# The last token group's output and query products on whole float32 operands instead of rounded high and low halves

## The chip, the cores and the metric

The kernel runs on one core of one Trainium2 chip. The metric is the device time of one execution in microseconds (us); less is better. A core has a matrix engine (TensorE, in the profile PE; its weight loads are PEld), a vector engine (VectorE, DVE), an activation engine (ScalarE, ACT), GpSimd (POOL) and SyncE (SP), which issues most transfers. Each engine takes its instructions in the order in which they stand in its queue.

## The reference, cut to what matters

One decoder layer over 1024 tokens of width 1024: a layer norm, a mixer of eight attention heads and four recurrent heads, an output projection, a layer norm, and PEER retrieval over 16384 experts, of which each token uses 128.

```python
mixed = jnp.concatenate([fox_o, h_o], axis=-1)
mix = mixed @ w_out                                  # output product, 1024 x 1024
x = _layer_norm(DEEPNORM_ALPHA * x + mix, ...)
q = (xt @ w_q).reshape(T, PEER_HEADS, 2, PEER_HALF)  # query product, 1024 x 2048
s = jnp.einsum('thpd,hpnd->thpn', q, sub_keys)
s_top, i_top = lax.top_k(s, PEER_TOPK)               # 16 of 128, per head and half
```

All of it is float32.

## The kernel before

The tokens go through the mixer in three groups (`GROUPS`): tokens 0 to 255, 256 to 767 and 768 to 1023. For each group the kernel runs the attention (`fox`) and the recurrence (`hgrn`), then the output product and the layer norm (`mix_out`), then the query product, the scores and their top 16 (`select`). This text is about the last group, 256 tokens.

A product of two float32 matrices is made of three matrix products in the format float32r, which keeps fewer bits (`mm3`). A weight tile of 128x1024 comes from memory (`wraw`); ScalarE rounds it (`whi`), and another engine forms the rest (`wlo`) by a subtraction. For the last group `WDIV` gives 1 for both products, which sends every such subtraction to GpSimd:

```python
nc.scalar.activation(hi, raw, AF.Copy)
self.nw += 1
eng = nc.vector if not WDIV[k] or self.nw % WDIV[k] else nc.gpsimd
eng.tensor_tensor(lo, raw, hi.bitcast(F32), op=ALU.subtract)
```

The other operand is held in `mh` and `ml`, the same two halves of the mixer's output and later of its layer norm; `ml` is formed by VectorE wherever `mh` is written. `mm3` adds high by high, high by low and low by high. The last group's output product takes 8 weight tiles, 64 products of 128x128 by 128x256 counted without their halves; its query product takes 16 tiles and 128 products. The raw tiles have 3 buffers, the halves 3 each (`WRAW`, `weight`). Products that are not split, such as the attention's logits (line 667), its sums over values (line 704) and the scores (line 822), are fed with whole float32 operands already.

While the last group is in its mixer, output product and selection, another job runs between its steps: `gbuild` writes the gates of four token blocks (`DENSE`) as a dense matrix `d_g`. It has 64 steps of eight tokens. In a step VectorE makes 16-bit one-hot tiles of 128x1024 (line 947: `ohi`, `ohj`, `ah`, `al`; every other step ScalarE makes `ah`), TensorE multiplies them (lines 972 and 974), and ScalarE copies the result to `slab`. Four steps fill a slab of 2 MB, of which there is one buffer; it must be written out before the next is begun. `tick` decides how many of these steps are put between two steps of the main work, by the constants `RATE`, in the program's text, not at run time. What is left of them when the selection is issued is drained after it.

After that the dense stage begins (`dense`): all 16384 experts for the four dense blocks as matrix products, and beside it the rest of the gather of expert rows for the other blocks. It is not touched. The order of instructions on each engine is fixed when the program is built; tiles are given places in the on-chip memory as pools open and close on its left and right side, and a load into a place waits for the last use of what was there.

Of the kernel before, what the change touches and what calls it, by code (L numbers as in the profile page):

```python
# [8 lines left out]
F32 = mybir.dt.float32  # L9
F32R = mybir.dt.float32r  # L10
# [5 lines left out]
ALU = mybir.AluOpType  # L16
# [4 lines left out]
P = 128  # L21
DC = D // P
# [30 lines left out]
FPOST = {256: 2, 512: 2}  # L53
WRAW = {"p0": 3, "m0": 3, "s0": 3, "p1": 3, "m1": 3, "s1": 3, "m2": 3, "s2": 3}
EARLY = 0
LNB = {256: 0, 512: 2}
HKD, HXK, HSB = 1, (), ()
PLAG = 1
# [13 lines left out]
class Layer:  # L72
# [130 lines left out]

    def weight(self, wp, src, k):
        nc = self.nc
        raw = wp.tile([P, 1024], F32, name="wraw", tag="wraw", bufs=WRAW[k])
        hi = wp.tile([P, 1024], F32R, name="whi", tag="whi", bufs=3)
        lo = wp.tile([P, 1024], F32R, name="wlo", tag="wlo", bufs=3)
        self.q("w").dma_start(raw, src)
# [4 lines that stand above are left out]
        return hi, lo  # L214
# [49 lines left out]
    def transpose_split(self, st, src, hi, lo, t, pool=None):  # L264
        nc = self.nc
        sl = slice(t * P, (t + 1) * P)
        for c0 in range(0, DC, 4):
            pt = self.bank(st)
            for c in range(4):
                nc.tensor.transpose(pt[:, c * P : (c + 1) * P], src[:, (c0 + c) * P : (c0 + c + 1) * P], self.ident)  # L270
            v = pt.rearrange("p (c t) -> p c t", c=4)
            h = hi[:, c0 : c0 + 4, sl]
            nc.scalar.activation(h, v, AF.Copy)
            if pool:
                x = pool.tile([P, 4, P], F32, name="tsx", tag="tsx", bufs=2)
                nc.scalar.activation(x, v, AF.Copy)
                nc.gpsimd.tensor_tensor(lo[:, c0 : c0 + 4, sl], x, h.bitcast(F32), op=ALU.subtract)
            else:
                nc.vector.tensor_tensor(lo[:, c0 : c0 + 4, sl], v, h.bitcast(F32), op=ALU.subtract)

    def mm3(self, out, lh, ll, rh, rl, start, stop, **kw):
        mm = self.nc.tensor.matmul
        mm(out, lh, rh, start=start, stop=False, **kw)  # L283
        mm(out, lh, rl, start=False, stop=False, **kw)  # L284
        mm(out, ll, rh, start=False, stop=stop, **kw)  # L285

    def projT(self, w, xh, xl, T):
        wh, wl = (t.rearrange("p (c m) -> p c m", c=DC) for t in w)
        out = []
        for c0 in range(0, T, 512):  # L290
            c = min(T - c0, 512)
            po = self.bank("h" if c0 else "f")[:, :c]
            for dc in range(DC):
                self.mm3(po, wh[:, dc], wl[:, dc], xh[:, dc, c0 : c0 + c], xl[:, dc, c0 : c0 + c], dc == 0, dc == DC - 1)
            out.append((slice(c0, c0 + c), po))
        return out

    def projN(self, wp, name, g, xh, xl, nq, k):
        po = [self.bank("h" if n == 2 else "f").rearrange("p (b n) -> p b n", b=2) for n in range(nq // 2)]
        for half in range(2):  # L300
            w = self.weight(wp, self.a[name][g, half], k)
            wh, wl = (t.rearrange("p (c n) -> p c n", c=4) for t in w)
            for tb in range(nq):
                for c in range(4):
                    dc = half * 4 + c
                    ts = slice(tb * P, (tb + 1) * P)
                    self.mm3(po[tb // 2][:, tb % 2], xh[:, dc, ts], xl[:, dc, ts], wh[:, c], wl[:, c],
                             dc == 0 and tb % 2 == 0, dc == DC - 1, skip_group_check=True)
        return po

    def mixers(self, groups, es):
        st, gb, tl = ExitStack(), ExitStack(), ExitStack()
        self.lx = ExitStack()
        init = self.setup()
        next(init)
        x1 = self.project(*groups[0], st)
        next(init)
        for n, (t0, T) in enumerate(groups):
            nq = T // P
            late = n + 1 == len(groups)  # L320
            if n < 2:
                self.project_cols(t0, T if n == 0 else S - t0, *x1)
            st.close()
            if n < 2:
                tl.close()
            po = st.enter_context(self.pool("po", 1, "left"))
            mh = po.tile([P, DC, T], F32R, name="mh", tag="mh")
            ml = po.tile([P, DC, T], F32R, name="ml", tag="ml")
            with self.pool("pf", 1, "left") as pf, self.pool("pk", 2, "left") as pk, \
                    self.pool("pg", 2, "left") as pg:  # L330
                fx = self.fox(t0, T, mh, ml, pf, pk)
                hg = self.hgrn(t0, T, mh, ml, pg)
                for _ in range(nq):
                    next(hg)
                    for i in range(8 // nq):
                        if i == HPOST[T]:
                            next(hg)
                        next(fx)
                    if HPOST[T] >= 8 // nq:
                        next(hg)  # L340
                    self.tick("hgrn", T)
            self.mix_out(t0, T, mh, ml)
            while late and not self.tailed:
                next(self.bjobs[0])
            pz = self.pz if late else tl.enter_context(self.pool("pz", 1, "right"))
            sv = pz.tile([P, nq, 16, 16], F32, name="sv", tag="sv")
            si = pz.tile([P, nq, 16, 16], U32, name="si", tag="si")
            best = pz.tile([P, nq, 8, 16], F32, name="best", tag="best")
            pos = pz.tile([P, nq, 8, 16], U32, name="pos", tag="pos")
            if n == 0:  # L350
                x1 = self.preload(T, S - T)
            self.select(t0, T, mh, ml, sv, si, best, pos, T == 256 or EARLY)
            if late:
                self.drain(self.bjobs)
                gb.close()
                st.close()
                while self.nv < sum(b not in VDVE for b in GATHER):
                    self.tick("dense")
                self.hx.close()
                dense = self.dense_prep(es)  # L360
            pw = tl.enter_context(self.pool("pw", 1, "right"))
            if n == 0:
                x1 = self.project(T, S - T, st, x1)
                self.lx.close()
            tail = self.select_tail(t0, T, sv, si, best, pos, T == 256 or EARLY, pw)
            if T == 256:
                tail = self.tail_gather(t0, T, tail)
                if late:
                    return dense, tail, tl
                self.drain([tail])  # L370
                self.hold = HOLD
            else:
                self.tailed = False
                self.bjobs.append(self.tail_gbuild(tail, tl, gb))
# [114 lines left out]
    def hgrn(self, t0, T, mh, ml, pg):  # L489
        nc = self.nc  # L490
# [7 lines left out]
        for ck in range(T // P):  # L498
            r0 = t0 + ck * P
            rs = slice(r0, r0 + P)  # L500
            q, f, v, k, lf = t4("q", QB[T]), t4("f", QB[T]), t4("v", QB[T]), t4("k", 2), t4("lf")
# [40 lines left out]
            for li, c in ((-2, 64), (-1, 32), (0, 16), (1, 8), (2, 4), (3, 2)):  # L542
# [12 lines left out]
                                        op=ALU.mult)  # L555
# [15 lines left out]
                else:  # L571
# [4 lines left out]
                                    op=ALU.mult)  # L576
# [9 lines left out]
            pt = b4()  # L586
# [12 lines left out]
            for h in range(4):  # L599
                nc.vector.scalar_tensor_tensor(self.state[:, h], self.state[:, h], eb[:, h : h + 1], pst[:, h],  # L600
                                               op0=ALU.mult, op1=ALU.add)
# [16 lines left out]
            pt = b4()  # L618
            for h in range(4):
                nc.tensor.transpose(pt[:, h], ov[:, h], self.ident)  # L620
            sl = slice(ck * P, (ck + 1) * P)
            nc.scalar.activation(mh[:, 4:8, sl], pt, AF.Copy)
            nc.vector.tensor_tensor(ml[:, 4:8, sl], pt, mh[:, 4:8, sl].bitcast(F32), op=ALU.subtract)
            yield

    def fox(self, t0, T, mh, ml, pf, pk):
        nc = self.nc
# [58 lines left out]
        def mixv(h, prs):  # L686
            p, e = divmod(h, 2)
# [27 lines left out]
            if e == 1:  # L715
# [8 lines left out]
                def post():  # L724
                    po = self.bank("f")[:, :T]
                    for qb in range(nq):
                        nc.tensor.transpose(po[:, qb * P : (qb + 1) * P], o[:, qb], self.ident)
                    g = self.foxg[:, p : p + 1]
                    nc.scalar.activation(mh[:, p], po, AF.Copy, scale=g)
                    nc.vector.scalar_tensor_tensor(ml[:, p], po, g, mh[:, p].bitcast(F32), op0=ALU.mult, op1=ALU.subtract)  # L730
                    self.dump("mh", mh[:, p].bitcast(F32), lambda d: d[p * P : (p + 1) * P, t0 : t0 + T])

                if FPOST[T] and h < 7:
# [568 lines left out]
```

## Time and profile before

| | |
|---|---|
| median of 3 runs | 3122.69 us (3122.61 to 3125.11) |
| the profiled execution, its time | 3098.22 us |
| its span | 3096.5 us |
| busy PE / PEld / DVE / ACT / POOL | 2614.4 / 2150.2 / 2707.3 / 1097.2 / 1678.8 us |
| mean granted clock of TensorE | 0.918 of full speed |

The profiled execution was 24.5 us faster than the median of the timed runs; all rows below come from it. Times in rows are us from the start of the span, unless marked ns. A row of a timeline with a count of x5 stands for five instructions in a row; an instruction's duration reaches into that of the next where the engine overlaps them, so a pace is read from start to start.

### The profile page before, as it was taken

The numbers are of one execution on the slowest core, as the hardware profiler recorded it, in microseconds if no ns is written. First come the engines' busy times: TensorE is split into PE (matmuls) and PEld (weight loads), VectorE is DVE, ScalarE is ACT, GpSimd is POOL, SyncE is SP. The second block draws the span as 40 slices with busy tenths as digits, with TensorE's granted clock in tenths as the row PEclk, the third lists the DMA queues.
The fourth block names the chain that finished last, engine by engine and source line by source line (L and its number), as shares of the span: only waits on it lengthen the run. The fifth ranks groups of instructions, "written<-read, shape, count | busy, mean of one in ns | idle before, by whom it ended". The sixth has DMA issues, their size and how long they took to land.

```text
span 3096.5 us, 45624 instructions
## 1 busy us (share of the span) xinstructions
PE 2614.4 (84%) x16057; PEld 2150.2 (69%) x16057; DVE 2707.3 (87%) x5573; ACT 1097.2 (35%) x2028; POOL 1678.8 (54%) x1240
## 2 busy tenths in 40 slices
PE   6778799777779768777569999899989999999995
PEld 6768589755566545666457778687768877877874
DVE  8658766588769998989798999899999999999998
ACT  4733222365222433766322223232323322222331
POOL 2344377655656644433046666565567665656652
PEclk9878899898889889879689999999999999999997
DMA  7632599754978858763489999999999999999994
GB/s 269 198 137 89 184 336 330 241 162 151 350 253 290 290 164 298 256 249 144 186 280 342 346 377 360 340 366 361 350 344 367 381 379 357 357 370 342 370 336 159
DMA packets 338662, 887.13 MB, mean 286 GB/s; under 512 B 29912, under 2 KB 124136, under 8 KB 336000
## 3 DMA queue, kind: packets, MB, share of 16 engines
q0 software_dynamic: 147456, 536.94, 47.5%
q1 hardware_dynamic: 185200, 338.38, 31.3%
q10 hardware_dynamic: 5776, 8.90, 0.8%
q8 instruction: 126, 2.06, 0.3%
q14 instruction: 104, 0.85, 0.1%
HBM read 821.67 MB, written 62.42 MB: 286 GB/s over the span
## 4 chain that ended last, share of the span: by engine, by line
DVE 40%; PE 36%; issue 11%; DMA 6%; ACT 4%; POOL 3%; SPq 0%; DVEq 0%; POOLq 0%; ACTq 0%
DVE ys L1134 8%; DVE rows L1109 6%; PE psf L284 6%; PE psf L285 5%; PE psf L283 5%; PE psh L285 4%; PE psh L283 4%; PE psh L284 4%; DMA rows<-in_v,gsel 2%; POOL rows L1090 2%; DVE dy L1049 2%; DVE vl L1017 1%; DVE ohj L947 1%; DVE tw L793 1%; DVE al L947 1%
## 5 line engine op out<-in xcount | busy, mean ns | idle before, releaser
L1090 POOL DMA_INDIRECT rows<-in_u,gsel x512 | 689.7, 1347 | 481.8 <-DVE rows L1109 302.5
L1090 POOL DMA_INDIRECT rows<-in_v,gsel x512 | 637.9, 1246 | 433.3 <-DVE ys L1134 264.5
L1109 DVE SCALAR_TENSOR_TENSOR rows<-rows,gx 128x1024 f32<-128x1024 f32 x512 | 629.8, 1278 | 38.6 <-DMA rows<-in_u,gsel 25.3
L1134 DVE SCALAR_TENSOR_TENSOR ys<-rows,sd,ys 128x1024 f32<-128x1024 f32 x381 | 491.2, 1289 | 0.6
L283 PE MATMUL psh<-dxh,uh 128*128 128x512 f32 x1024 | 402.8, 393 | 28.9 <-ACT uh L1016 16.1
L285 PE MATMUL psh<-dxh,ul 128*128 128x512 f32 x1024 | 400.8, 391 | 9.5 <-DVE ul L1017 9.4
L284 PE MATMUL psh<-dxl,uh 128*128 128x512 f32 x1024 | 400.3, 391 | 0.0
L284 PE MATMUL psf<-vl,hh 128*128 128x512 f32 x768 | 312.3, 407 | 42.9 <-DVE vl L1017 42.1
L1016 ACT ACTIVATE vh<-vr 128x512 fp32r<-128x512 f32 x256 | 161.8, 632 | 435.8 <-PE psv L285 408.7
L285 PE MATMUL psf<-vh,hl 128*128 128x512 f32 x768 | 307.7, 401 | 0.0
L283 PE MATMUL psf<-vh,hh 128*128 128x512 f32 x768 | 279.1, 395 | 11.9 <-DVE dy L1049 9.7
L1016 ACT ACTIVATE uh<-ur 128x1024 fp32r<-128x1024 f32 x128 | 136.0, 1062 | 410.6 <-PE psh L284 408.9
L213 POOL TENSOR_TENSOR wlo<-wraw,whi 128x1024 fp32r<-128x1024 f32 x70 | 181.8, 2603 | 154.1 <-ACT whi L210 145.7
L283 PEld LDWEIGHTS psh<-dxh,uh 128*128 128x128 f32 x1024 | 193.5, 189 | 76.8 <-ACT hs L1030 20.3
L285 PEld LDWEIGHTS psh<-dxh,ul 128*128 128x128 f32 x1024 | 193.4, 189 | 50.6 <-DVE ul L1017 10.5
L210 ACT ACTIVATE whi<-wraw 128x1024 fp32r<-128x1024 f32 x130 | 136.9, 1056 | 250.8 <-PE psf L284 64.1
L284 PEld LDWEIGHTS psh<-dxl,uh 128*128 128x128 f32 x1024 | 193.6, 189 | 39.7
L284 PEld LDWEIGHTS psf<-vl,hh 128*128 128x128 f32 x768 | 148.7, 194 | 90.2 <-DVE vl L1017 59.4
L1017 DVE TENSOR_TENSOR vl<-vr,vh 128x512 fp32r<-128x512 f32 x256 | 170.6, 688 | 14.0 <-ACT vh L1016 13.9
L283 PEld LDWEIGHTS psf<-vh,hh 128*128 128x128 f32 x768 | 145.5, 190 | 50.1 <-DVE dy L1049 10.0
L213 DVE TENSOR_TENSOR wlo<-wraw,whi 128x1024 fp32r<-128x1024 f32 x60 | 81.8, 1365 | 111.0 <-ACT whi L210 111.0
L285 PEld LDWEIGHTS psf<-vh,hl 128*128 128x128 f32 x768 | 149.1, 194 | 30.2
(337 smaller groups left out, 6354.4 us busy)
## 6 DMA issues: line engine op xcount, KB each, us to landing
ur<-in_ut SPq DMA_DIRECT2D x128, 512.0 KB
vr<-in_v SPq DMA_DIRECT2D x256, 256.0 KB
d_g<-slab SPq DMA_DIRECT2D x16, 2048.0 KB
gt<-d_g SPq DMA_DIRECT2D x32, 1024.0 KB
wraw<-in_wq SPq DMA_DIRECT2D x48, 512.0 KB
wraw<-in_wt SPq DMA_DIRECT2D x34, 512.0 KB
wraw<-in_wn SPq DMA_DIRECT2D x24, 512.0 KB
wraw<-in_wo SPq DMA_DIRECT2D x24, 512.0 KB
```

The source lines that it names most:

```text
L210: nc.scalar.activation(hi, raw, AF.Copy)
L213: eng.tensor_tensor(lo, raw, hi.bitcast(F32), op=ALU.subtract)
L283: mm(out, lh, rh, start=start, stop=False, **kw)
L284: mm(out, lh, rl, start=False, stop=False, **kw)
L285: mm(out, ll, rh, start=False, stop=stop, **kw)
L947: eng.tensor_tensor(t.rearrange("p t (m c) -> p t m c", c=2), x, y, op=op)
L1016: nc.scalar.activation(hi, raw, AF.Copy)
L1017: nc.vector.tensor_tensor(lo, raw, hi.bitcast(F32), op=ALU.subtract)
L1049: nc.vector.tensor_tensor(y[:, tb, ns], y[:, tb, ns], acc[tb], op=ALU.add)
L1090: self.nc.gpsimd.indirect_dma_start(out=t, out_offset=None, in_=tab, in_offset=bass.IndirectOffsetOnAxis(ap=idx, axis=0))
L1109: self.pin(nc.vector.scalar_tensor_tensor(u, u, 1.0, x2, op0=ALU.mult, op1=ALU.mult, accum_out=sd[:, n : n + 1]), "u")
L1134: self.pin(nc.vector.scalar_tensor_tensor(ys, v, h, ys, op0=ALU.mult, op1=ALU.add), "w")
```

## The change

The last group's two products, `m2` and `s2`, are named in a table `WHOLE` with the number of buffers of their raw tiles, 5 and 6. For them `weight` issues the load alone; `mm3` issues one matrix product on the raw tile and on an `mh` of type float32; `ml` isn't allotted, and the four places that form it are skipped. The other two groups are as before.

```diff
+WHOLE = {"m2": 5, "s2": 6}
...
     def weight(self, wp, src, k):
         nc = self.nc
+        if k in WHOLE:
+            raw = wp.tile([P, 1024], F32, name="wraw", tag="wraw", bufs=WHOLE[k])
+            self.q("w").dma_start(raw, src)
+            return raw, None
...
             nc.scalar.activation(h, v, AF.Copy)
+            if lo is None:
+                continue
...
     def mm3(self, out, lh, ll, rh, rl, start, stop, **kw):
         mm = self.nc.tensor.matmul
+        if ll is None:
+            mm(out, lh, rh, start=start, stop=stop, **kw)
+            return
         mm(out, lh, rh, start=start, stop=False, **kw)
...
-            mh = po.tile([P, DC, T], F32R, name="mh", tag="mh")
-            ml = po.tile([P, DC, T], F32R, name="ml", tag="ml")
+            whole = f"m{n}" in WHOLE
+            mh = po.tile([P, DC, T], F32 if whole else F32R, name="mh", tag="mh")
+            ml = None if whole else po.tile([P, DC, T], F32R, name="ml", tag="ml")
...
-            nc.vector.tensor_tensor(ml[:, 4:8, sl], pt, mh[:, 4:8, sl].bitcast(F32), op=ALU.subtract)
+            if ml is not None:
+                nc.vector.tensor_tensor(ml[:, 4:8, sl], pt, mh[:, 4:8, sl].bitcast(F32), op=ALU.subtract)
```

On POOL's queue, at the end of the last group's mixer, this stood before; `rows<-in_v` and `rows<-in_u` are gathers of expert rows, and the last row is the gather that follows the selection.

```order
L1090 DMA rows<-in_v,gsel 128x1024
L213 TENSOR_TENSOR wlo<-wraw,whi 128x1024 x7
L1090 DMA rows<-in_u,gsel 128x1024 x2
L213 TENSOR_TENSOR wlo<-wraw,whi 128x1024
L1090 DMA rows<-in_u,gsel 128x1024 x2
L261 TENSOR_TENSOR rows<-rows 128x1024
L1090 DMA rows<-in_u,gsel 128x1024 x3
L213 TENSOR_TENSOR wlo<-wraw,whi 128x1024 x16
L1090 DMA rows<-in_u,gsel 128x1024 x176
```

The same place on POOL's queue now:

```order
L1090 DMA rows<-in_v,gsel 128x1024
L1090 DMA rows<-in_u,gsel 128x1024 x4
L261 TENSOR_TENSOR rows<-rows 128x1024
L1090 DMA rows<-in_u,gsel 128x1024 x179
```

All 24 subtractions of weight tiles are gone, and three gathers have moved behind the one addition that stays.

On SP's queue, from the last loads of the attention (`k<-d_c`) to the first load of an output weight (`wraw<-in_wo`), this stood before; `kt` holds the sub-keys, `wraw<-in_wq` are the query weights, `gsl` is what `gbuild` reads.

```order
L644 DMA k<-d_c 1x1024
L218 DMA ln_mix_g<-in_ln_mix_g 128x1024
L218 DMA ln_mix_b<-in_ln_mix_b 128x1024
L920 DMA d_sel<-sel 128x384
L768 DMA res<-d_x_76 128x1024 x2
L920 DMA d_sel<-sel 128x384
L931 DMA gsl<-d_sel 128x384 x3
L980 DMA d_g<-slab 128x4096
L209 DMA wraw<-in_wo 128x1024 x7
```

The same stretch of SP's queue now:

```order
L658 DMA k<-d_c 1x1024
L818 DMA kt<-in_kt 128x2048
L935 DMA d_sel<-sel 128x384
L209 DMA wraw<-in_wq 128x1024 x6
L935 DMA d_sel<-sel 128x384
L946 DMA gsl<-d_sel 128x384 x3
L995 DMA d_g<-slab 128x4096
L223 DMA ln_mix_g<-in_ln_mix_g 128x1024
L223 DMA ln_mix_b<-in_ln_mix_b 128x1024
L783 DMA res<-d_x_76 128x1024 x2
L209 DMA wraw<-in_wo 128x1024 x2
```

The sub-keys and the first six query weights have moved from behind the layer norm to ahead of the output product, and the layer norm's constants and `res` from ahead of the first slab to behind it.

## Rows read from the trace of the kernel before

**Rows 1.** Busy us (instructions) of each engine by stretch, clock, DMA share, GB/s.

```profile
1056.00:1256.00 200.00, 143.97 (x1576) 95.23 (x1574) 175.12 (x681) 86.45 (x244) 93.57 (x99) 0.88 0.73 243
1256.00:1345.00 89.00, 61.17 (x594) 52.37 (x594) 80.77 (x130) 64.05 (x153) 33.02 (x17) 0.82 0.76 283
1345.00:1450.00 105.00, 87.50 (x764) 81.49 (x765) 99.49 (x333) 72.40 (x177) 48.52 (x16) 0.90 0.47 179
1450.00:1512.00 62.00, 30.88 (x274) 25.23 (x271) 62.00 (x226) 22.96 (x42) 0.00 (x0) 0.63 0.35 144
1600.00:3096.00 1496.00, 1403.74 (x5999) 1133.83 (x5997) 1438.28 (x1945) 428.90 (x630) 914.93 (x677) 0.97 0.95 348
```

**Rows 2.** POOL in order of time: start us, us, idle before and its releaser.

```profile
1263.24 14.11 POOL L213 TENSOR_TENSOR wlo<-wraw,whi 128x1024 fp32r<-128x1024 f32 x5 [3.82 <-ACT whi L210]
...
1403.77 4.88 POOL L213 TENSOR_TENSOR wlo<-wraw,whi 128x1024 fp32r<-128x1024 f32 x1 [7.13 <-ACT whi L210]
```

**Rows 3.** DVE in order of time, at the first split of a weight.

```profile
1263.22 0.69 DVE L947 TENSOR_TENSOR al<-ohi,gpair 128x1024 f16<-128x1024 f16 x1
1263.94 2.73 DVE L947 TENSOR_TENSOR ohi<-iota16h,gpair 128x1024 f16<-128x1024 f16 x1
1266.58 2.89 DVE L947 TENSOR_TENSOR ohj<-iota16h,gpair 128x1024 f16<-128x1024 f16 x1
1269.40 2.89 DVE L947 TENSOR_TENSOR al<-ohi,gpair 128x1024 f16<-128x1024 f16 x1
```

**Rows 4.** Line 947 alone by stretch: DVE busy us (instructions), clock, DMA.

```profile
1256.00:1345.00 89.00, 59.00 (x70) 0.82 0.76 283
1345.00:1450.00 105.00, 60.92 (x73) 0.90 0.47 179
1450.00:1512.00 62.00, 40.47 (x65) 0.63 0.35 144
```

**Rows 5.** Line 833 alone by stretch, the same columns.

```profile
1345.00:1450.00 105.00, 6.39 (x20) 0.90 0.47 179
1450.00:1512.00 62.00, 2.04 (x12) 0.63 0.35 144
```

**Rows 6.** Instructions of the tile ml: ns min/median/max, first and last start.

```profile
L279 DVE TENSOR_TENSOR ml<-psf,mh x16: 675/683/692, 235.0 to 1334.3; 128x512 fp32r<-128x512 f32 x16
L730 DVE SCALAR_TENSOR_TENSOR ml<-psf,foxg,mh x12: 475/484/752, 157.6 to 1257.7; 128x256 fp32r<-128x256 f32 x8, 128x512 fp32r<-128x512 f32 x4
```

**Rows 7.** Waits of DVE, 1200 to 1512 us: total, times, longest.

```profile
DVE ah L947 <- PE psh L972: 11.5, 4, 4.2
```

**Rows 8.** The chain that ended last, 1300 to 1360 us: start, us, what.

```profile
1333.76 6.39 DMA wraw<-in_wq
...
1345.29 2.65 POOL wlo L213
```

**Rows 9.** SP's issues in order of time, 1300 to 1345 us.

```profile
1312.42 0.32 SPq L980 DMA_DIRECT2D d_g<-slab  x1
...
1328.20 0.32 SPq L980 DMA_DIRECT2D d_g<-slab  x1
...
1342.55 0.33 SPq L980 DMA_DIRECT2D d_g<-slab  x1
```

**Rows 10.** PE in order of time, products of rounded halves.

```profile
1266.50 0.27 PE L283 MATMUL psf<-whi,mh 128*128 128x256 f32 x1
1266.62 0.28 PE L284 MATMUL psf<-wlo,mh 128*128 128x256 f32 x1
```

**Rows 11.** PE in order of time, products of whole float32 operands.

```profile
1206.37 1.60 PE L704 MATMUL psv<-v,pt 128*128 128x128 f32 x12
1207.82 0.27 PE L701 MATMUL psf<-ident,pr 128*128 128x128 f32 x1
1207.92 1.02 PE L667 MATMUL psf<-k,q 65*128 65x512 f32 x2
1208.79 0.39 PE L704 MATMUL psv<-v,pt 128*128 128x128 f32 x2
```

More of the change, by code (lines that the diff above doesn't have):

```diff
@@ L287, in projT @@
     def projT(self, w, xh, xl, T):
-        wh, wl = (t.rearrange("p (c m) -> p c m", c=DC) for t in w)
+        wh, wl = (t if t is None else t.rearrange("p (c m) -> p c m", c=DC) for t in w)
+        lo = lambda t, *i: None if t is None else t[(slice(None), *i)]
         out = []
@@ L293, in projT @@
             for dc in range(DC):
-                self.mm3(po, wh[:, dc], wl[:, dc], xh[:, dc, c0 : c0 + c], xl[:, dc, c0 : c0 + c], dc == 0, dc == DC - 1)
+                self.mm3(po, wh[:, dc], lo(wl, dc), xh[:, dc, c0 : c0 + c], lo(xl, dc, slice(c0, c0 + c)), dc == 0, dc == DC - 1)
             out.append((slice(c0, c0 + c), po))
@@ L301, in projN @@
             w = self.weight(wp, self.a[name][g, half], k)
-            wh, wl = (t.rearrange("p (c n) -> p c n", c=4) for t in w)
+            wh, wl = (t if t is None else t.rearrange("p (c n) -> p c n", c=4) for t in w)
+            lo = lambda t, *i: None if t is None else t[(slice(None), *i)]
             for tb in range(nq):
@@ L306, in projN @@
                     ts = slice(tb * P, (tb + 1) * P)
-                    self.mm3(po[tb // 2][:, tb % 2], xh[:, dc, ts], xl[:, dc, ts], wh[:, c], wl[:, c],
+                    self.mm3(po[tb // 2][:, tb % 2], xh[:, dc, ts], lo(xl, dc, ts), wh[:, c], lo(wl, c),
                              dc == 0 and tb % 2 == 0, dc == DC - 1, skip_group_check=True)
@@ L729, in post @@
                     nc.scalar.activation(mh[:, p], po, AF.Copy, scale=g)
-                    nc.vector.scalar_tensor_tensor(ml[:, p], po, g, mh[:, p].bitcast(F32), op0=ALU.mult, op1=ALU.subtract)
+                    if ml is not None:
+                        nc.vector.scalar_tensor_tensor(ml[:, p], po, g, mh[:, p].bitcast(F32), op0=ALU.mult, op1=ALU.subtract)
                     self.dump("mh", mh[:, p].bitcast(F32), lambda d: d[p * P : (p + 1) * P, t0 : t0 + T])
```

## The prediction

> **What bounds the kernel now.** I read the busy time by stretch first [rows 1]. The last group's attention and recurrence lie in 1056 to 1256 us, its output product and layer norm in 1256 to 1345, its query product in 1345 to 1450, and what is left of the top 16 and of `gbuild` in 1450 to 1512; the dense stage follows. The reader is to see that from 1256 on DVE is the fullest engine: 80.77, 99.49 and 62.00 us of 89, 105 and 62, that is 242.3 of 256, idle 13.7. PE is busy 179.6 of them, ACT and POOL less. So the 256 us end when DVE's work ends, and what the change is worth here is what it takes off DVE, not off PE.
>
> Then I asked why DVE needs so long. In its order of time [rows 3] an instruction of line 947 takes 0.69 us; the next three, of the same line and size, take 2.73 to 2.89 us. Beside them [rows 2] POOL runs five subtractions `wlo` from 1263.24 on, 14.11 us, 2.8 us each. The slow stretch begins when POOL does, and each slow instruction is about as long as one subtraction. Later it can be the other way round: the `wlo` at 1403.77 takes 4.88 us itself. Line 947 by stretch [rows 4] gives the size: 65 instructions in 40.47 us, 0.623 each, where no `wlo` runs; 70 in 59.00 and 73 in 60.92 where 24 of them do.
>
> In the Trainium skill, "SBUF — State Buffer", Who interferes with whom, says that a VectorE instruction with two inputs in the on-chip memory and a GpSimd instruction that reads it exclude each other, whichever comes second waiting for the other's end. The trace agrees, in both directions. By that rule each of the 24 costs one of the two engines up to a whole 2.8 us, 67 us if all fell on DVE; the rows below show half of it on DVE.
>
> The other views are for what might stop a faster DVE: its own waits, in which 11.5 us go to `ah`, four times for PE [rows 7]; the chain, in which the first query weight's load and split stand after the layer norm [rows 8]; and SP's issues of slabs [rows 9].
>
> **The change part by part.**
>
> *Subtractions off POOL.* All 24 go. On DVE line 947 loses 59.00 - 70 x 0.623 = 15.4 us in the second stretch and 60.92 - 73 x 0.623 = 15.4 in the third [rows 4]. Line 833 also has two inputs in memory: 20 instructions in 6.39 us against 12 in 2.04 [rows 5], so 6.39 - 20 x 0.17 = 3.0. Together 33.8 us. The bound below is nothing, if the coincidence in time were chance; above it nothing more is to be had, since only excess over the undisturbed stretch is counted.
>
> *`ml` off DVE.* Between 1256 and 1345 one instruction of 0.48 us and four of 0.68 [rows 6], 3.2 us. In the mixer before them two on the recurrence's side, like the four, and three like the one: 2.8 us.
>
> *Roundings off ACT.* 24 `whi`. ACT is busy 64.05 and 72.40 us of 89 and 105 [rows 1], so I count nothing for them; the DVE work above covers it. The same holds for POOL's time.
>
> *Whole products on PE.* 192 triples become 192 single products. A product of rounded halves starts 0.12 us after the one before (1266.50, 1266.62) [rows 10]: 0.36 a triple at the full clock. The trace has no whole product of 256 columns. It shows two instructions for each whole product: with 128 columns twelve from 1206.37 to 1207.82, 0.121 each, 0.242 a product; with 512 columns two from 1207.92 to 1208.79, 0.87 [rows 11]. These are the bounds; on a line between them 256 columns give 0.45, by columns from the larger 0.435. I take 0.44. PE's work then grows by 192 x 0.08 = 15 us (bounds: -23 and +98), to 195 us beside DVE's 205. It is hidden behind DVE while PE has this room; if DVE weren't there, 15 us would be the loss.
>
> In the Trainium skill, "FP8 and Floating Point Precision", TensorE Precision Notes, a true float32 product takes four passes through the array. At 0.12 us a pass that would be 0.48, or 192 x 0.12 = 23 us more for PE; the rows say the same within a tenth. It speaks against the change, and would decide if PE were the bound.
>
> *The loads moved ahead.* `kt` (1 MB) and six query weights (3 MB) now stand among the last attention loads, four transfers of 0.5 MB move away from there. Net 2 MB at the 243 GB/s of that stretch [rows 1] is 0 to 9 us for gathers that PE's queue waits for; with the 2.8 us of `ml` won there I take nothing for the two. Later, the query weights are there when the layer norm ends. Now the first one lands 6.39 us after 1333.76 and its split ends at 1347.9 [rows 8]. DVE fills most of this with `gbuild`, so the 14 us aren't added to the sum; they take away idle time.
>
> *DVE's idle time.* 13.7 us now. Waits for split weights on PE go. What is late next is the slab: without any split running, slabs are issued 15.8 and 14.4 us apart (1312.42, 1328.20, 1342.55) [rows 9], while four `gbuild` steps cost DVE 14 instructions, 8.7 us. A slab has one buffer, so in the output product DVE can't run at its own pace. Five slabs at 15 us are 75 us where the second stretch takes 89: that stretch gains 14, not the 18.6 of the parts above. I put 3 us on the idle time for this; bounds: the 13.7 vanish, or 17 more come (rival B).
>
> Sum: 33.8 + 3.2 - 3 = 34 us. The dense stage is as full as before on DVE and PE (1438 and 1404 of 1496 us [rows 1]) and begins earlier by that. The profiled execution took 3098.22 us, so 3064; the timed median is 24.5 us above it, and I take the same 34 us off: 3122.69 - 34 = **3089 us**.
>
> **The rivals.**
>
> A, the forecast: 3089, with the idle bounds 3072 to 3101.
>
> B, PE's queue takes a good part back. PE runs in order; in the output product 16 whole products, 7.0 us, stand in a block between two `gbuild` steps, and DVE has two buffers ahead. If each of the four blocks makes DVE wait as long as its longest wait for PE now, 4.2 us [rows 7], 17 us are lost: 3106. For it: the waits of that kind exist. Against: the triples took 5.8 us there and waited for splits besides.
>
> C, nothing to be seen: the slow instructions of line 947 owe their length to something else, or slabs bind the query stretch too. There line 947 has 73 instructions [rows 4], 14 to a slab, so some five slabs in 105 us, 21 us each, well over 15, so this has little for it: 3123.
>
> D, slower. TensorE falls to the lower of its two clock levels, 1.2 GHz, for these products. In 1450 to 1512 the granted clock is 0.63 with PE half idle; in the two product stretches it is 0.82 and 0.90 [rows 1]. At half the clock a whole product is 0.88 us, 192 x (0.88 - 0.36) = 100 us more, and PE's 179.6 become 280 of 256: 24 us later than now, 3147. It decides once PE's growth passes the 76 us that PE now stands idle. Against it: PE has more to do in one piece than before, and where it was fullest the clock was highest.
>
> That whole operands run as one short pass is excluded by [rows 11]; even then PE, which isn't the bound, would gain alone.
>
> **How the numbers follow.** A 0.66; more than A, with the idle time gone and the moved loads for free, 0.05; B 0.16; C 0.07; D 0.06. A measurement of this kernel tells about 0.2%, 6.2 us, from no change. Faster by more: 0.66 + 0.05 + 0.16 = 0.87; within it 0.07; slower 0.06. The range 3066 to 3114 takes in A with its bounds, B and some 8 us beyond it, and leaves out C, D and most of the case above A.
>
> **What would show it.** Right: no instruction of line 947's kind over 1 us between the mixer's end and the drain, 0.62 us each throughout; DVE busy about 205 us there; the stretch from the mixer's end to the last `dxl` some 34 us shorter; whole products at 0.44 us. Wrong: long waits of DVE for PE on `ah`, or of ACT for a slab, in the same stretch; a clock under 0.8 in the products; gathers of rows that land later in the attention; a dense stage longer than 1496 us for the same window of work.

## The result, and the profile after

The changed kernel takes 3102.66 us (median of 4 runs, 3096.88 to 3103.77) beside 3123.9 us of the kernel before: a ratio of 0.9927, 95% interval 0.991 to 0.9945. A second measurement gave 0.9932 (0.9905 to 0.9958). So it is faster by about 0.7%, 21 us by the medians; 34 were forecast.

The two profiled executions don't show it: 3098.22 before, 3096.88 after. They spent very different times in the last group's attention, 219.5 and 249.2 us. This is not the change: the kernel before, traced once more, took 251.8 there (first experiment). So all stages below are cut at marks of each trace's own: the last `mh` of the attention (line 743, 1284.4 us in the trace after), the last transpose of the layer norm's rows (1364.6, cut at 1365.1), the last query product (1461.3), the first `dxl` (1516.5). From the first mark to the last the kernel before takes 254.2 us in one trace and 254.6 in the other, the changed one 232.1 and 231.7. That is 22 us, as much as the whole gain.

Busy time of each engine by stretch, the changed kernel; the columns are those of [rows 1].

```profile
1284.40:1365.10 80.70, 59.95 (x481) 48.09 (x482) 54.61 (x113) 49.38 (x127) 10.68 (x9) 0.88 0.73 280
1365.10:1461.30 96.20, 90.58 (x728) 76.82 (x728) 92.44 (x367) 66.24 (x182) 0.00 (x0) 1.00 0.53 198
1461.30:1516.50 55.20, 27.63 (x230) 23.12 (x228) 55.20 (x201) 20.20 (x36) 0.00 (x0) 0.62 0.38 157
```

The same three stretches in the second trace of the kernel before:

```profile
1291.70:1369.20 77.50, 54.91 (x527) 48.18 (x524) 70.76 (x115) 54.83 (x131) 32.38 (x17) 0.83 0.76 275
1369.20:1483.60 114.40, 93.85 (x827) 86.47 (x825) 105.00 (x336) 79.32 (x193) 48.78 (x16) 0.87 0.52 196
1483.60:1546.30 62.70, 31.38 (x279) 25.76 (x277) 62.70 (x235) 24.36 (x44) 0.00 (x0) 0.67 0.34 139
```

The reader is to see two things. DVE, the third pair, has 202.25 us of work in place of 238.47, 36.2 less. And its idle time has grown, from 254.6 - 238.47 = 16.1 to 232.1 - 202.25 = 29.9 us, of which 26.1 lie in the first stretch (6.7 before): there DVE has 16 us less to do, and the stretch is 3 us longer. The query stretch and the drain give 18 and 7.5 us.

DVE's work fell where it was expected. Line 947 is line 962 now; alone, by stretch, in the changed kernel:

```profile
1284.40:1365.10 80.70, 37.11 (x59) 0.88 0.73 280
1365.10:1461.30 96.20, 54.39 (x89) 1.00 0.53 198
1461.30:1516.50 55.20, 36.45 (x60) 0.62 0.38 157
```

That is 0.63, 0.61 and 0.61 us each: the 2.7 us instructions of [rows 3] are gone, and the stretches with products look as the drain of [rows 4] did.

What DVE waits for in these 232.1 us (total, times, longest):

```profile
DVE res L790 <- PE psf L291: 9.7, 2, 5.3
DVE ah L962 <- PE psh L987: 9.6, 6, 3.2
DVE sv L807 <- ACT s L840: 2.0, 1, 2.0
DVE rows L1228 <- ACT rows L1199: 1.9, 1, 1.9
DVE gs__14892 L950 <- DMA gsl<-d_sel: 1.8, 1, 1.8
DVE ohi L962 <- ACT ah L973: 1.5, 2, 0.8
DVE rows L265 <- ACT rows L264: 1.3, 1, 1.3
DVE ohj L962 <- PE psh L989: 1.2, 2, 0.9
```

The second was there before: 11.5 us in [rows 7], 12.9 in the second trace. The first is new; it was 0.2 us. `res` is the addition of the output product to the residual, and line 291 the whole product. All waits for TensorE together (`res`, `ah`, `ohj`) are 20.5 us, where the second trace of the kernel before has 14.3; in the first stretch alone they are 19.7 and were 5.2. The five rows that wait for ScalarE or a transfer add 8.5 us, where that trace has 0.8. TensorE and DVE in order of time, where the new wait ends:

```profile
1296.02 7.17 PE L291 MATMUL psf<-wraw,mh 128*128 128x256 f32 x32 [1.84 <-DMA wraw<-in_wo]
1303.13 1.07 PE L1177 MATMUL y<-rows,hTm 128*32 128x256 f32 x16
...
1305.04 7.12 PE L291 MATMUL psf<-wraw,mh 128*128 128x256 f32 x32
...
1303.24 0.69 DVE L790 SCALAR_TENSOR_TENSOR res<-res,psf 128x512 f32<-128x512 f32 x1 [5.27 <-PE psf L291]
1312.20 0.69 DVE L790 SCALAR_TENSOR_TENSOR res<-res,psf 128x512 f32<-128x512 f32 x1 [4.40 <-PE psf L291]
```

Sixteen products, 32 hardware instructions, take 7.17 us by the row, 0.448 us each, and 7.11 from start to start (1296.02 to 1303.13), 0.444 each. While they run TensorE does no tables' products, so that no buffer of DVE's comes free, and next in DVE's order is the addition that needs the sixteen.

### The profile page after: what moved, and what is told of

Read it like the earlier page. It is cut to its first block, busy times and chain, and to the rows that moved or that the text cites. A ratio compares the mean times of both kernels' runs of the same rounds, so it can differ in the third digit from the quotient of the medians.

```text
span 3094.9 us, 45136 instructions
## 1 busy us (share of the span) xinstructions
PE 2628.0 (85%) x15865; PEld 2150.5 (69%) x15865; DVE 2664.9 (86%) x5563; ACT 1076.2 (35%) x2004; POOL 1614.0 (52%) x1216
## 5 line engine op out<-in xcount | busy, mean ns | idle before, releaser
L1124 DVE SCALAR_TENSOR_TENSOR rows<-rows,gx 128x1024 f32<-128x1024 f32 x512 | 627.9, 1273 | 40.7 <-DMA rows<-in_u,gsel 20.5
L293 PE MATMUL psh<-dxh,uh 128*128 128x512 f32 x1024 | 402.9, 393 | 29.4 <-ACT uh L1031 16.5
L293 PEld LDWEIGHTS psh<-dxh,uh 128*128 128x128 f32 x1024 | 193.5, 189 | 77.2 <-ACT hs L1045 19.1
L215 ACT ACTIVATE whi<-wraw 128x1024 fp32r<-128x1024 f32 x106 | 111.5, 1056 | 231.5 <-issue 62.8
L295 PEld LDWEIGHTS psf<-vh,hl 128*128 128x128 f32 x768 | 147.9, 193 | 29.9
L1032 DVE TENSOR_TENSOR ul<-ur,uh 128x1024 fp32r<-128x1024 f32 x128 | 156.2, 1221 | 12.3 <-ACT uh L1031 11.2
```

The lines of the kernel that those rows point to most:

```text
L1032: nc.vector.tensor_tensor(lo, raw, hi.bitcast(F32), op=ALU.subtract)
L1124: self.pin(nc.vector.scalar_tensor_tensor(u, u, 1.0, x2, op0=ALU.mult, op1=ALU.mult, accum_out=sd[:, n : n + 1]), "u")
```

## Experiments

Each kernel is told by its ratio to the kernel before on the same chip, and by its trace between the marks above. The numbers in one place, in us; "output" is the output product with its layer norm, "rest" the query stretch and the drain. The two pairs of traces of one kernel agree within 0.4 us in the sum:

```
                          ratio (95%)             output  rest   sum    DVE busy  DVE idle
before                    1                        75.8   178.4  254.2   240.5     13.7
before, second trace      1                        77.5   177.1  254.6   238.5     16.1
changed                   0.9927 (0.9910-0.9945)   80.7   151.4  232.1   202.3     29.9
changed, second trace     0.9932 (0.9905-0.9958)   80.2   151.5  231.7   202.5     29.2
ml kept                   0.9946 (0.9926-0.9965)   82.9   151.3  234.2   205.9     28.3
POOL busy again           0.9977 (0.9958-0.9996)   84.0   161.7  245.7   218.7     27.0
query products only       0.9929 (0.9916-0.9943)   73.9   161.6  235.5   219.5     16.0
output product only       0.9980 (0.9969-0.9991)   76.9   174.0  250.9   226.6     24.3
half the output products  one run                  68.5   158.2  226.7   203.5     23.2
a third buffer            0.9943 (0.9928-0.9958)   80.7   153.3  234.0   204.7     29.3
half slabs                0.9979 (0.9958-0.9999)   96.1   138.7  234.8   204.4     30.4
before, half slabs        1.0075 (1.0051-1.0099)   99.3   156.4  255.7   241.6     14.1
query only, half slabs    1.0004 (0.9988-1.0020)  101.6   143.5  245.1   221.5     23.6
query only, wlo on DVE    0.9954 (0.9935-0.9972)   78.8   160.8  239.6   212.7     26.9
```

**The kernel before once more**, unchanged, and **the changed kernel once more**. With the changed kernel's first trace at hand I had two theories for its long attention: that dropping `ml` let the scheduler place some rows of TensorE otherwise there, at a cost of some 25 us (theory 1), or that this stretch differs between executions (theory 2).

> The kernel before, once more, for a second trace: the first one was of an execution of 3098 us, 25 us under the timed median. Theory 1 (the change made the last attention slower): its stretch from the second group's last query product to the last `mh` of the attention is again about 220 us, and the 25 us that the first trace lacks lie elsewhere. Theory 2 (that stretch varies from one execution to the next): it is nearer to the 249 us of the changed kernel's trace.

> The changed kernel, once more. Time 3102 both ways, ratio 0.993. Theory 1: the last group's mixer takes 245 to 250 us again. Theory 2: it comes out well below, 220 to 235, since 249 was one slow execution.

The kernel before took 251.8 us from the second group's last query product to the attention's end, the changed one 252.9. Theory 1 has fallen, since the kernel before is as slow there. Theory 2 missed as well: it had the changed kernel at 220 to 235 us, by chance of the execution, and this trace is as slow as the first. The kernel before in its first trace and in its second, this stretch alone:

```profile
1037.70:1257.20 219.50, 152.48 (x1636) 100.00 (x1638) 194.48 (x765) 95.71 (x262) 103.86 (x109) 0.87 0.76 251
```

```profile
1039.90:1291.70 251.80, 176.39 (x1636) 112.94 (x1638) 192.16 (x762) 97.28 (x262) 103.03 (x109) 0.79 0.67 217
```

The same instructions, at a granted clock of 0.87 and 0.79. Of all thirteen later traces (the changed kernel's first one among them) five lie at 217.6 to 223.5 us, eight at 248.8 to 259.1, and the kernels that ran in one session, each session on a chip of its own, all lie on the same side. So what decides goes with the session or the chip.

**`ml` kept.** The same theory from the other side.

```diff
-            ml = None if whole else po.tile([P, DC, T], F32R, name="ml", tag="ml")
+            ml = po.tile([P, DC, T], F32 if whole else F32R, name="ml", tag="ml")
-        if ll is None:
+        if ll is None or rl is None:
```

> The changed kernel, but `ml` of the last group is still computed on DVE (and read by nothing). With it TensorE's rows of the last attention stand in the order of the kernel before; without it 58 rows are placed otherwise. Theory 1 (that order costs 25 us): the mixer takes about 222 us, and the time is 3080 (3070 to 3088), in spite of 6 us more DVE work. Theory 2 (the order does nothing): 3103 to 3108, the mixer as long as in the changed kernel.

The mixer took 255.7 us, and theory 1 had 222. Instruction by instruction, TensorE's order in it differs from the kernel before in 3 places, and from the changed kernel in some 150. The ratio is 0.9946, 0.0014 or 4 us above the changed kernel's, with intervals that overlap; DVE is busy 3.4 us longer between the marks. `ml`'s own work accounts for that: the order of those rows is worth nothing that can be measured.

**POOL busy again.**

```diff
             self.q("w").dma_start(raw, src)
+            x = wp.tile([P, 1024], F32, name="wx", tag="wx", bufs=1)
+            nc.gpsimd.tensor_tensor(x, raw, raw, op=ALU.subtract)
             return raw, None
```

> The changed kernel with 24 subtractions of a weight from itself put back on POOL, their result read by nothing; products stay whole. If the length of line 947's instructions comes from POOL's subtractions: these are 2.7 us beside them again, the same 30 us more of DVE time, of which the query stretch shows 15 to 20 in the time (3118 to 3122), the output product less, since DVE stands idle there for 26 us. If their length had another cause: 3102, 0.62 us each.

The ratio went back to 0.9977: of the 21 us that the changed kernel gained on this chip (0.0068 of 3126.64), 14 are gone (0.0045). Line 962 (964 here) between the first mark and the last query product, by tile:

```profile
L964 DVE TENSOR_TENSOR ohj<-iota16h,gpair 128x1024 f16<-128x1024 f16 x42 | 36.7, 875 | 0.2
L964 DVE TENSOR_TENSOR ohi<-iota16h,gpair 128x1024 f16<-128x1024 f16 x42 | 34.1, 813 | 1.8 <-ACT ah L975 1.5
```

In the changed kernel the mean of either is 0.68 us; here it is 0.88 and 0.81 (`al` and `ah`: 0.72 and 0.73). One of them beside POOL, in order of time:

```profile
1394.87 4.19 POOL L211 TENSOR_TENSOR wx<-wraw 128x1024 f32<-128x1024 f32 x2 [42.73 <-DMA wraw<-in_wq]
...
1395.83 1.48 DVE L964 TENSOR_TENSOR ah<-ohi,gpair 128x1024 f16<-128x1024 f16 x1 [0.57 <-PE psh L989]
```

So it is POOL's subtraction that lengthens DVE's instruction, whatever TensorE does with the weight. It gives back 16.5 us of DVE time, not 30: a subtraction takes 2.1 us here where `wlo` took 2.7 in the median, and 6 of the 24 run ahead of the first mark, with the early loads. The time, 3120.15 us, lies in the expected 3118 to 3122, but that was worked out from twice the DVE time, so the hit is luck. The 18 subtractions between the marks are 37.2 us of POOL's time, and 16.5 of them fall on DVE. In the Trainium skill, "SBUF — State Buffer", Who interferes with whom, a VectorE instruction with two inputs in the on-chip memory and a GpSimd instruction that reads it exclude each other. The trace agrees: 1.48 us beside POOL in place of 0.68. Two thirds of the gain are shown by this to hang on POOL's subtractions. The last third (`wlo`'s greater length, `ml`, the waits for split weights) isn't told apart.

**Each part alone.**

```diff
-WHOLE = {"m2": 5, "s2": 6}
+WHOLE = {"s2": 6}
```

and in the other kernel `{"m2": 5}`; in both the query product's operand has a tile of its own, since the output product's is of the other kind.

> Only the query products on whole operands, the output product on halves as before. By the traces so far all of the gain lies in the query stretch and the drain (177 us before, 151.5 after), and the output product and layer norm take 77 to 78 us on halves against 80 whole. So 3100 to 3105 where the kernel before takes 3126.6, a little better than the whole change. Rival (the parts add up, each worth its subtractions): some 3115.

> Only the output product on whole operands. If its gain of DVE time turns into waiting: output product and layer norm 80 us, query stretch and drain 177 us as before, time 3126 to 3130, nothing gained. Rival (the parts add up): 3113 to 3117.

The query products alone give the whole gain by the ratio, 0.9929; between the marks they give 19 of the 22 us. The output product alone gives 0.2%, 6 us, between the two expectations. DVE has 12 us less to do than in the second trace of before, 14 less than in the first; the output stretch stayed at 76.9 us, and 8 of the 12, 11 of the 14, became idle time.

**Half the output products**, **a third buffer**, **half slabs.** Why doesn't the output stretch get shorter? Theory P: TensorE's blocks of sixteen whole products. Theory S: the one slab buffer.

```diff
                     dc = half * 4 + c
+                    if k == "m2" and c % 2:
+                        continue
...
```

(The line left out ends the sum with the last product that stays.)

> The changed kernel without every second one of the 64 whole products of the last group's output product, so its output lacks half of that product. Theory P (DVE waits because TensorE does 16 whole products, 7.1 us, in a block before the next tables' products): blocks of 8 take 3.5 us, and output product and layer norm fall from 80 us to 66 to 70, DVE's idle time there from 26 to 14 us or less. Theory S (the one slab buffer and its transfer set the pace there): 77 to 80 us as it is.

The stretch falls to 68.5 us, as P has it, and DVE's idle time in it to 17.0, where P had 14 or less. But the query stretch and the drain take 6.7 us longer, and DVE's idle time as a whole falls by only 6 us, from 29.2 to 23.2. So TensorE's products bound the length of the output stretch; that is not the same as bounding the whole, since the tables' work that is not done in it is done later.

```diff
-                        t = pool.tile([P, 8, P], F16, name=name, tag=name, bufs=2)
+                        t = pool.tile([P, 8, P], F16, name=name, tag=name, bufs=3)
-                        ah = pool.tile([P, 8, P], F16, name="ah", tag="ah", bufs=2)
+                        ah = pool.tile([P, 8, P], F16, name="ah", tag="ah", bufs=3)
```

> The changed kernel with a third buffer for each of the four one-hot tiles of line 962, so that DVE can work one step more ahead of TensorE. Theory P: the stretch of output product and layer norm falls from 80 us to 70 to 75, and the time by 5 to 10 us, to 3097 to 3102. Theory S: DVE runs ahead once, 2.5 us, and no more: 3104 to 3107.

80.7 us and 234.0 in all: nothing. DVE's wait for `ah` became one for `ohj`, 7.0 us in the output stretch, and `res` still waited 6.9.

```diff
-                slab[0] = pool.tile([P, P, 32], F32, name="slab", tag="slab", bufs=self.slabs)
+                slab[0] = pool.tile([P, P, 16], F32, name="slab", tag="slab", bufs=self.slabs)
-        self.nw, self.slabs = 0, 1
+        self.nw, self.slabs = 0, 2
```

(with the DRAM tile, the transfer and the tile that reads it back cut in the same way)

> The changed kernel with slabs of half the size in two buffers (32 transfers of 1 MB in place of 16 of 2 MB, the same bytes and the same memory), so that the next slab can be filled while one is on its way. Theory S (one slab buffer sets the pace from the end of the attention to the first `dxl`, 232 us, 16.4 us a slab): DVE's idle 29 us there shrink to 15 or less and the 232 us fall to 215 to 222. Theory P (TensorE's blocks of whole products make DVE wait): 229 to 233 as it is. The dense stage reads the slabs back in runs of 256 bytes in place of 512, which may cost it something; so the verdict is read from the stretch, and the ratio to the kernel before lies between 0.988 (S, dense stage untouched) and 0.995 or more.

> The kernel before with the same half slabs. Both theories: DVE is the bound there (240 of 254 us busy), so the stretch falls by no more than its idle 14 us, to 245 to 252; the dense stage shows what the shorter runs cost (1585 us without them).

> Query products whole, output product on halves, and half slabs. Theory S: from 235.5 us to 222 to 228, less than the whole change gains from them, since POOL's subtractions still lengthen DVE's work in the output product. Theory P: 233 to 236.

The stretch from mark to mark took 234.8 us, and the kernel before with half slabs 255.7, which both theories had at 245 to 252: nothing there. More tables are built during the output product and fewer after it, and the sum stays. What DVE waits for in the changed kernel with half slabs:

```profile
DVE res L790 <- DMA wraw<-in_wo: 10.7, 1, 10.7
DVE sv L807 <- ACT s L840: 5.1, 2, 3.7
DVE res L790 <- PE psf L291: 5.0, 1, 5.0
```

A new wait has come in: the first output product's weight lands later. So S as I stated it fell, but the experiment doesn't prove that the slab costs nothing. The third kernel, with the query products alone, did worse in the stretch (245.1) than S or P had it. All three are 0.5 to 0.75% slower than without half slabs. Their profiled executions were 12 us faster, 18 us faster and 5 us slower than their medians, and only the last shows a longer dense stage (1596 us where the other kernels have 1573 to 1587). Where the rest is lost is not settled.

**The output product's `wlo` on DVE**, with the query products whole.

```diff
-WDIV = {"p0": 0, "m0": 1, "s0": 1, "p1": 3, "m1": 2, "s1": 2, "m2": 1, "s2": 1}
+WDIV = {"p0": 0, "m0": 1, "s0": 1, "p1": 3, "m1": 2, "s1": 2, "m2": 0, "s2": 1}
```

> Query products whole, output product on halves, and the eight subtractions `wlo` of the output product on DVE in place of POOL. If POOL's subtractions lengthen line 947's instructions by 14 us in the output product: they are 0.62 us there too, DVE does 8 x 1.22 = 9.8 us more of its own, net 4 us less; the stretch from the attention's end to the first `dxl` goes from 235.5 us to 229 to 234, the ratio to the kernel before from 0.993 to 0.991 to 0.993. Rival (the length has another cause, or PE waits for split weights behind DVE's other work): DVE's 9.8 us come on top, 240 to 246 us, ratio 0.995 to 0.997.

The DVE part came as the first theory has it: line 967 (962 in the changed kernel) takes 38.22 us for 59 instructions in the output stretch, 0.65 each, where with the query products alone it took 49.75 for 55; and DVE as a whole 64.49 in place of 69.04. The time came as the rival has it, or nearly: 239.6 us, 0.9954. The output stretch:

```profile
1248.30:1327.10 78.80, 56.98 (x543) 49.35 (x544) 64.49 (x122) 56.84 (x134) 11.34 (x9) 0.85 0.69 261
```

Here no product is whole, and yet DVE stands idle for 14.3 of 78.8 us. TensorE's wait for a split weight behind DVE, which the rival names, is there, 3.3 us, but DVE's own waits for the tables' products are longer, 8.9. So neither theory was right as a whole: DVE's work in the output stretch can be had for less, but it buys nothing.

## Why the prediction was right, and where not

The direction was right, the time lay in the range, and the gain was two thirds of the forecast. But 3102.66 lies outside the bounds of A itself, 3072 to 3101, and inside the range because that takes in rival B. (The upper of these bounds is misadded: with 17 us more of idle time it is 3122.69 - 37 + 17 = 3103.) Step by step:

*DVE sets the end, and POOL lengthens its instructions.* The first half held in the query stretch and the drain: the query products alone took 19.0 us of work off DVE and 19.1 off the time between the marks. It failed in the output product, which alone took 11.9 and 3.7 (both against the second trace of before). The second half is right, and its size too. Line 947 lost 156.71 - 127.95 = 28.8 us against the second trace of before, 31.4 against the first; 30.8 were forecast. All of DVE lost 36 to 38 us; 33.8 + 3.2 = 37 were forecast. The POOL experiment shows the cause.

*Whole products at 0.44 us.* They take 0.444 to 0.448 in a block of sixteen. (The estimate from the Trainium skill, "FP8 and Floating Point Precision", TensorE Precision Notes, 0.48 by four passes, was 7 to 8% too much.) TensorE's busy time nevertheless did not grow by 15 us: it is 178.2 us between the marks, and was 178.8 and 180.2. The 0.36 us for a triple was read where the clock was full; in the query stretch the clock was 0.88 or 0.87 before and is 1.00 now, so the triples had cost more than that in the mean: counted from each start to the next start or the product's own end, 0.46 us each in the first trace of before (58.8 us for 128), as much as a whole product now (59.4 for 128). This also is the end of rival D: where the products stand the clock rose.

*The loads that moved ahead.* The attention took 249.2 and 252.9 us beside 251.8, so no loss shows there, as assumed. It isn't excluded: on the chip with the short attention, two variants with both products whole took 223.2 and 223.5 us, and those with one of them 218.1 and 217.6. The dense stage is as long as before, 1578 and 1585 us beside 1585 and 1583.

*DVE's idle time.* This step failed. I wrote that the slab would keep the output stretch from gaining more than 14 us and put 3 us on it. The stretch gained nothing, it lost 3, and idle time grew by 13.7 us against the second trace of before (16 against the first). 37 less 3 was 34; 36.2 less 13.7 is 22.5. Five slabs at 15 us was the wrong floor: it asked how fast slabs can follow each other, not when TensorE gets to them. SP's issues of slabs in the output stretch of the changed kernel, and what ScalarE waits for a slab's transfer there:

```profile
1292.44 0.33 SPq L995 DMA_DIRECT2D d_g<-slab  x1
...
1320.69 0.33 SPq L995 DMA_DIRECT2D d_g<-slab  x1
...
1337.28 0.32 SPq L995 DMA_DIRECT2D d_g<-slab  x1
...
1353.79 0.32 SPq L995 DMA_DIRECT2D d_g<-slab  x1
...
ACT slab L992 <- DMA d_g<-slab: 11.9, 4, 4.9
```

The first gap is 28.3 us, and the two blocks of whole products shown above, with DVE's two waits for them, lie in it; the next two are 16.6 and 16.5 us, near the 15 assumed. ScalarE's wait for a slab, which the prediction names as a sign that it is wrong, was 4.6 and 5.1 us in the two traces of before. With whole or split products, with two or three buffers, the output stretch took 74 to 84 us, and DVE's work in it could be anything from 54 to 72 us; half slabs made it longer still. Before, that floor and DVE's work lay together (71.6 of 75.8 us busy), which made DVE look like the bound of both stretches.

*Rival B* gave 3106 and comes nearest to the time, and its waits are there, on `res` more than on `ah`: in the output stretch DVE's waits for TensorE grew by 14.5 us (19.7 beside 5.2), where B had 17. Over the whole they grew by 6 only (20.5 beside 14.3); the rest of the new idle time is short waits for ScalarE and transfers. And only part of them is due to what B names. Taking away half of the whole products took 6 us off the idle time; with no whole product in the output stretch at all, but with less DVE work, 14 us of idle time stayed in it. What sets the floor of the output stretch, beyond TensorE's products, is open. The remaining candidates are the layer norm's chain behind the products and the slab, with the load of the first weight; they weren't separated.

*Time of before.* I took the same 34 us off two numbers that were 24.5 us apart, without asking where the 24.5 lay. As far as the traces show it was in the attention, outside the change, so the subtraction was sound; but the trace that I read was of another pace than the timed runs.

None of the variants beats the change clearly. The query products alone come out level with it (0.9929), with half the edit.

## What to carry to other kernels

When an edit takes work off the fullest engine, ask for each stretch apart what would end it if that engine did nothing at all; a share of 95% busy can be two limits that lie together, and then work taken off turns into waiting. A subtraction put on GpSimd is not free because GpSimd is idle: look at what VectorE's own instructions take beside it. And cut two traces at events of the program, not at times, before comparing them: here 30 us that belonged to neither kernel hid the whole gain.

## What the runs showed of the hardware that was not expected

The same kernel differs by 1% between sessions, each on a chip of its own: medians of 3126.64, 3125.03, 3095.31 and 3091.62 us for the kernel before. In the traces the difference lies almost wholly in one stage, the last group's mixer, 217.6 to 223.5 us (granted clock 0.84 to 0.87, six traces) and 248.8 to 259.1 (0.78 to 0.81, eight traces); the dense stage after it takes 1573 to 1587 us on both sides, but for the one of 1596. Twelve products of the attention in the first trace of before, and twelve in the changed kernel's:

```profile
1159.56 1.60 PE L704 MATMUL psv<-v,pt 128*128 128x128 f32 x12
```

```profile
1249.03 2.44 PE L718 MATMUL psv<-v,pt 128*128 128x128 f32 x12 [2.09 <-ACT pt L716]
```

The first stand right behind other products, and the granted clock is 1.00 from 1159.5 to 1161.2 us. The second stand behind a pause of 2.09 us, and the clock is 0.62 from 1249.0 to 1251.5. TensorE is busy for 152 to 160 us of the stage in the six traces and for 171 to 180 in the eight. Why the clock is lower in one session than in another, the traces don't show.
